# A squared-ReLU MLP whose second product is made by Strassen's seven products for two of three token groups

## The chip, the cores and the metric

One core of a Trainium2 chip runs the whole program. The metric is the time of one execution on the device in microseconds (us); lower is better. The engines are named as the profile names them: PE (matrix products; PEld is its weight load), DVE, ACT and POOL (elementwise work), SP (issues transfers). A row such as `128x512 f32` is 128 partitions by 512 elements each.

## The reference

A two-part layer over 2176 tokens (17 tiles of 128): a mixer (a gated recurrence and chunk-band attention), then the MLP. Only the MLP is touched, and it is about half of the time:

```
x = x + concat(o_h, o_a) @ w_out
u = rmsnorm(x, norm2_g) @ w_up            # 1024 -> 4096
x = x + square(relu(u)) @ w_down          # 4096 -> 1024
y = rmsnorm(x, final_norm_g)
```

All data are float32. Every product of two matrices is made as three: each operand is split into a rounded part (`hi`) and the rest (`lo`), and hi·hi, hi·lo and lo·hi are summed (`mm3`, L365). A split is one cast on ACT and one subtraction on DVE (`wsplit`, L313, for weights).

## The kernel before

The mixer writes its output x1 to device memory and the MLP (`phase_mlp`, L1145) works through the tokens in three groups of 6, 6 and 5 tiles (`GROUPS_M`, L31). The group's normalised activations lie transposed and split in SBUF (`h_hi`, `h_lo`); `prepare` (L1096) makes them, for the first group beside the last of the mixer's output projection, for the others beside the group before.

Per group a loop runs over 16 slices of 256 of the 4096 hidden columns. One slice is:

- **up**: 4 PSUM groups (2 blocks of 128 columns by 2 halves of the tokens), each 24 matmuls of 384 columns (320 for the group of 5 tiles). ACT takes relu (L1178), DVE squares (L1179), ACT casts (L1181), DVE subtracts (L1182).
- **down**: for each token tile and each half of the 1024 output columns one PSUM group of 6 matmuls of 512 columns, which DVE adds to the accumulator y in SBUF (L1201).

Weights come from device memory as 512 KB pieces (`wraw`, two buffers) and are split into `whi`/`wlo` pieces of 512 columns, of which eight lie in SBUF; `wseq` (L344) loads one weight ahead of its use. The final norm of a finished tile (`finish`) is DVE's L125 and a store. Four PSUM buffers (`c.ps_mm`) rotate under up and down.

`weave` mixes two streams of work at trace time by given costs: the MLP of group 0 with the decode requests' attention (`sample_mixer`) and the preparation of group 1, the MLP of group 1 with the preparation of group 2. The order of the instructions on each engine is then fixed when the program is built: a scheduler walks a model of the engines and takes, of the instructions that are ready in it, the one that comes first in the program. So the order on an engine isn't the program's, but it doesn't change at run time either.

Of the kernel before, what the change touches and what calls it, by code (L numbers as in the profile page):

```python
# [17 lines left out]
P = 128  # L18
# [85 lines left out]
def rows(c, prompt, sample, t):  # L104
    return prompt[t * P:(t + 1) * P, :] if t < NPT else sample
# [179 lines left out]
    c.wsp = s.enter_context(c.tc.tile_pool(reuse_waits="tile", name="wsp", bufs=bufs))  # L285


RAW, PIECE = 1024, 512


class W:


    def __init__(self, c, w, ncol=WC, pool=None):
        nc = c.nc
        self.p = []
        self.kp = kp = PIECE // ncol
        for r0 in range(0, w.shape[1], RAW):
            raw = c.wraw.tile([P, RAW], F32, tag="wraw", name="wraw")
            nc.sync.dma_start(out=raw, in_=w[:, r0:r0 + RAW])  # L300
            for o in range(0, RAW, PIECE):
                rw = raw[:, o:o + PIECE]
# [5 lines left out]

    def lo(self, k, s):
        return self.p[k // self.kp][1][:, k % self.kp, s]  # L310


def wsplit(c, rw, pool=None):  # L313
# [7 lines left out]
    nc.scalar.copy(h, rw)  # L321
    nc.vector.tensor_tensor(out=l, in0=rw, in1=h.bitcast(F32), op=ALU.subtract)  # L322
    return hi, lo


class W2(W):
# [16 lines left out]

def wseq(c):  # L344

    srcs = []
    for _ in GROUPS:
        srcs += [(c.w_in[4:6], 0), (c.w_in[4:6], 1)] + [(c.w_in[i], WC) for i in (2, 3, 0, 1)] + \
            [(c.w_in[6:8], 0), (c.w_in[6:8], 1)]
    for kind, _ in TODO:  # L350
        srcs += [(c.w_in[i], WC) for i in (12, 8, 9, 10, 11, 13)] if kind == "p" else \
            [(c.w_out[i], WC) for i in range(D // WC)]
    for _ in GROUPS_M:
        for fc in range(DFF // WC):
            srcs += [(c.w_up[fc], WC), (c.w_down[fc, 0], 512), (c.w_down[fc, 1], 512)]
    w = W2(c, *srcs[0])
    yield None
    for x in srcs[1:]:
        nxt = (W2 if len(x[0].shape) == 3 else W)(c, *x)
        yield w  # L360
        w = nxt
    yield w


def mm3(c, ps, pairs, parts=1):  # L365
# [776 lines left out]
            yield 0.12 * w  # L1142


def phase_mlp(c):  # L1145
    tc, nc = c.tc, c.nc
    GMAX = max(len(g) for g in GROUPS_M) * P
    FC = WC
    with ExitStack() as s:
        def pool(name, bufs, **k):  # L1150
            return s.enter_context(tc.tile_pool(reuse_waits="tile", name=name, bufs=bufs, **k))
        cp = pool("m_const", 1)
        yp = pool("m_y", 7)
        up = pool("m_u", 1)
        wp = pool("m_u2", 2)
        c.ps_mm = pool("m_psmm", 4, space=PSUM)
        c.ps_tx, c.ps_tx_tag = pool("m_pstx", 2, space=PSUM), "tx"
        c.ps_smp = pool("m_pssmp", 2, space=PSUM)
        c.g2 = gain_tile(c, cp, "g2", c.norm2_g)
        gf = gain_tile(c, cp, "gf", c.final_g)  # L1160

        pend = []

        def finish(t, y):
            norm_rows(c, y, gf, y, "y")
            nc.sync.dma_start(out=rows(c, c.y_p, c.y_s, t), in_=y)

        def mlp(tiles, g):
            n = len(tiles) * P
            ys = []  # L1170
            for fc in range(DFF // FC):
                wu = next(c.ws)
                uh = up.tile([P, FC // P, GMAX], F32R, tag="uh", name="uh")
                ul = up.tile([P, FC // P, GMAX], F32R, tag="ul", name="ul")
                for f, cs, ps in proj_fm(c, wu, g, n, 1):
                    cn = cs.stop - cs.start
                    u2 = wp.tile([P, 384], F32, tag="u2", name="u2")[:, :cn]
                    nc.scalar.activation(u2, ps, AF.Relu)  # L1178
                    nc.vector.scalar_tensor_tensor(out=u2, in0=ps, scalar=0.0, in1=u2,  # L1179
                                                   op0=ALU.max, op1=ALU.mult)  # L1180
                    nc.scalar.copy(uh[:, f, cs], u2)  # L1181
                    nc.vector.tensor_tensor(out=ul[:, f, cs], in0=u2, in1=uh.bitcast(F32)[:, f, cs],  # L1182
                                            op=ALU.subtract)
                    for x in pend[:2]:
                        finish(*x)
                    del pend[:2]
                if not fc:
                    for t in tiles:
                        y = yp.tile([P, D], F32, tag="y", name="y")
                        nc.sync.dma_start(out=y, in_=c.x1[t * P:(t + 1) * P, :])  # L1190
                        ys.append(y)
                wd = [next(c.ws), next(c.ws)]
                full = slice(0, 512)
                for j, y in enumerate(ys):
                    ts = slice(j * P, (j + 1) * P)
                    for dc, w in enumerate(wd):
                        ps = c.ps_mm.tile([P, 512], F32, tag="mm", name="mm")
                        list(mm3(c, ps, [(uh[:, k, ts], ul[:, k, ts], w.hi(k, full), w.lo(k, full))
                                         for k in range(FC // P)]))
                        ysl = y[:, dc * 512:(dc + 1) * 512]  # L1200
                        nc.vector.tensor_tensor(out=ysl, in0=ps, in1=ysl, op=ALU.add)  # L1201
                    if fc == DFF // FC - 1:
                        if g.last and pend:
                            finish(*pend.pop())
                        pend.append((tiles[j], y))
                yield 1.0
            if g.last:
                finish(*pend.pop())

        h1 = Ctx()  # L1210
        c.h0.last = h1.last = False

        def side():
            yield from sample_mixer(c)
            h_tiles(pool("m_h", 1), h1)
            yield from prepare(c, GROUPS_M[1], h1)

        run(weave(mlp(GROUPS_M[0], c.h0), 17.0, side(), 26.0))
        run(weave(mlp(GROUPS_M[1], h1), 17.0, prepare(c, GROUPS_M[2], c.h0), 5.0))
        c.h0.last = True  # L1220
        run(mlp(GROUPS_M[2], c.h0))


@with_exitstack
def hymba_kernel(ctx, tc, x_prompt, x_sample, state_hgrn, cache_k, cache_v, lb_param, norm1_g, w_in,
# [19 lines left out]
    c.x1 = dram.tile([NTT * P, D], F32, name="x1")  # L1245
    c.sq, c.sk = (dram.tile([4, P, P], F32, name=x) for x in ("sq", "sk"))
    c.sv = dram.tile([P, 512], F32, name="sv")
    c.ws = wseq(c)
# [4 lines left out]
    wpools(c, ctx, 8, 2, 3)  # L1253
# [73 lines left out]
```

## Time and profile before

| | |
|---|---|
| median of 3 runs | 2972.8 us (2971.18 to 2977.19) |
| the profiled execution, its own time | 2972.54 us |
| its span, first to last instruction | 2970.8 us |
| around the span | 1.7 us |
| PE busy | 2891.7 us (97%) |
| DVE, ACT, POOL busy | 1752.2, 1111.0, 288.1 us |
| MLP's matmuls | from 1373.5 us to about 2957 us of the span |

The profiled execution lies 0.3 us under the median. A busy PE is not PE at its peak: matmuls overlap, so the price of one is the distance of the starts of two in a row, not its length.

### The profile page before, as it was taken

Reading aid. Unit: us, or ns where it says so; the run is one execution under the profiler, and the core shown is the slowest. Engines: PE = TensorE matmul, PEld = TensorE weight load, DVE = VectorE, ACT = ScalarE, POOL = GpSimd, SP = SyncE. Lnnn points to the kernel's source line nnn. Section 1 sums busy time; section 2 is a strip of 40 time slices with the busy share of each in tenths; the row PEclk is TensorE's granted clock in tenths of the full one; section 3 lists DMA queues with packets and bytes.
Section 4 is the critical chain, followed back from the end, with each engine's and each line's share of the span. In section 5 each row is a group of like instructions: output and inputs, shape, how many; then the busy total and the mean of one; then the engine's idle time right before and its main releaser. Section 6 shows DMA issues by size and latency. Waiting matters only on the chain.

```text
span 2970.8 us, 45500 instructions
## 1 busy us (share of the span) xinstructions
PE 2891.7 (97%) x18151; PEld 2626.6 (88%) x18151; DVE 1752.2 (59%) x3110; ACT 1111.0 (37%) x2256; POOL 288.1 (10%) x474
## 2 busy tenths in 40 slices
PE   8999999989999999998999999999999999999997
PEld 7888889889889899898888999999999999899997
DVE  5775775765556565656555555565555555555554
ACT  5433443435545455554223333332222223323222
POOL 3311321221010101011000000010000000000000
PEclk9999999999999999999999999999999999999999
DMA  7433323434333434447322332242212123222221
GB/s 268 163 126 113 113 97 102 137 107 140 100 125 107 128 106 140 141 156 268 114 85 87 117 98 79 72 148 65 78 57 71 57 71 128 82 75 73 84 72 64
DMA packets 119262, 328.06 MB, mean 110 GB/s; under 512 B 12613, under 2 KB 36937, under 8 KB 119050
## 3 DMA queue, kind: packets, MB, share of 16 engines
q1 hardware_dynamic: 110714, 299.20, 31.0%
q0 software_dynamic: 6320, 18.62, 1.6%
q10 hardware_dynamic: 2016, 7.34, 0.7%
q8 instruction: 142, 2.33, 0.3%
q14 instruction: 70, 0.57, 0.1%
HBM read 292.61 MB, written 32.51 MB: 109 GB/s over the span
## 4 chain that ended last, share of the span: by engine, by line
PE 73%; DVE 1%; ACT 1%; DMA 1%; issue 1%; POOL 0%; POOLq 0%; ACTq 0%; DVEq 0%
PE mm L370 22%; PE mm L372 21%; PE mm L371 21%; PE ps_oT L826 3%; PE S L819 2%; PE S L797 2%; PE tx L115 1%; ACT s L810 1%; PE ps_os L888 0%; DMA x<-x 0%; ACT junk L100 0%; DVE s L808 0%; PE tr L835 0%; ACT whi L321 0%; DVE wlo L322 0%
## 5 line engine op out<-in xcount | busy, mean ns | idle before, releaser
L321 ACT CAST whi<-wraw 128x512 fp32r<-128x512 f32 x816 | 498.0, 620 | 747.0 <-PE mm L372 537.2
L322 DVE TENSOR_TENSOR wlo<-wraw,whi 128x512 fp32r<-128x512 f32 x816 | 563.9, 708 | 238.2 <-ACT whi L321 234.3
L1201 DVE TENSOR_TENSOR y<-mm,y 128x512 f32<-128x512 f32 x544 | 373.7, 689 | 221.1 <-PE mm L372 219.4
L370 PE MATMUL mm<-h_hi,whi 128*128 128x384 f32 (+1 forms) x1536 | 503.2, 328 | 0.0
L372 PE MATMUL mm<-h_hi,wlo 128*128 128x384 f32 (+1 forms) x1536 | 501.5, 326 | 0.0
L371 PE MATMUL mm<-h_lo,whi 128*128 128x384 f32 (+1 forms) x1536 | 500.7, 326 | 0.0
L372 PE MATMUL mm<-whi,ul 128*128 128x512 f32 x1088 | 424.1, 390 | 0.0
L371 PE MATMUL mm<-wlo,uh 128*128 128x512 f32 x1088 | 424.0, 390 | 0.0
L370 PE MATMUL mm<-whi,uh 128*128 128x512 f32 x1088 | 423.5, 389 | 0.0
L370 PEld LDWEIGHTS mm<-h_hi,whi 128*128 128x128 f32 x1536 | 288.4, 188 | 4.7 <-issue 3.5
L371 PEld LDWEIGHTS mm<-h_lo,whi 128*128 128x128 f32 x1536 | 288.4, 188 | 1.2
L372 PEld LDWEIGHTS mm<-h_hi,wlo 128*128 128x128 f32 x1536 | 288.4, 188 | 0.0
L1179 DVE SCALAR_TENSOR_TENSOR u<-mm,u 128x384 f32<-128x384 f32 (+1 forms) x192 | 102.4, 534 | 278.4 <-ACT u L1178 278.3
L370 PE MATMUL mm<-hT_hi,whi 128*128 128x384 f32 (+1 forms) x768 | 259.7, 338 | 5.6 <-ACT qs L1003 4.1
L372 PE MATMUL mm<-hT_hi,wlo 128*128 128x384 f32 (+1 forms) x768 | 254.0, 331 | 0.2
L371 PE MATMUL mm<-hT_lo,whi 128*128 128x384 f32 (+1 forms) x768 | 253.4, 330 | 0.0
L372 PEld LDWEIGHTS mm<-whi,ul 128*128 128x128 f32 x1088 | 204.2, 188 | 43.1 <-DVE ul L1182 0.5
L370 PEld LDWEIGHTS mm<-whi,uh 128*128 128x128 f32 x1088 | 204.2, 188 | 41.7 <-ACT uh L1181 0.5
L371 PEld LDWEIGHTS mm<-wlo,uh 128*128 128x128 f32 x1088 | 204.2, 188 | 41.2
L1178 ACT ACTIVATE u<-mm 128x384 f32<-128x384 f32 (+1 forms) x192 | 90.4, 471 | 344.9 <-PE mm L372 344.9
L370 PE MATMUL mm<-whi,hT_hi 128*128 128x256 f32 x720 | 213.4, 296 | 0.5 <-ACT hT_hi L117 0.2
L90 POOL TENSOR_SCALAR r<-ss 128x1 f32<-128x1 f32 (+1 forms) x85 | 24.0, 283 | 1900.7 <-ACT junk L100 1675.7
(206 smaller groups left out, 4641.6 us busy)
## 6 DMA issues: line engine op xcount, KB each, us to landing
wraw<-in_w_in SPq DMA_DIRECT2D x168, 512.0 KB, 4.1
wraw<-in_w_up SPq DMA_DIRECT2D x96, 512.0 KB, 3.8
wraw<-in_w_down SPq DMA_DIRECT2D x96, 512.0 KB, 3.7
wraw<-in_w_out SPq DMA_DIRECT2D x48, 512.0 KB, 3.9
xT<-in_x_T SPq DMA_DIRECT2D x34, 512.0 KB, 4.2
og<-og SPq DMA_DIRECT2D x17, 512.0 KB, 3.5
x<-yo POOLq DMA_DIRECT2D x68, 128.0 KB, 3.3
x<-x SPq DMA_DIRECT2D x17, 512.0 KB, 4.7
```

What stands on the lines that cost most here:

```text
L115: nc.tensor.transpose(ps[:, k, :], src[:, (k0 + k) * P:(k0 + k + 1) * P], c.ident)
L321: nc.scalar.copy(h, rw)
L322: nc.vector.tensor_tensor(out=l, in0=rw, in1=h.bitcast(F32), op=ALU.subtract)
L370: nc.tensor.matmul(ps, lh, rh, start=(i == 0), stop=False)
L371: nc.tensor.matmul(ps, lh, rl, start=False, stop=False)
L372: nc.tensor.matmul(ps, ll, rh, start=False, stop=(i == n - 1))
L797: nc.tensor.matmul(S[:, bk, :n], a[es, qc], c.K[ft][es, b, kc], start=(a is q and not b), stop=(a is ql))
L819: nc.tensor.transpose(ps[:, x, :], s[:, x * P:(x + 1) * P], c.ident)
L826: nc.tensor.matmul(poT[64 * e:64 * e + 64, j, :], g.vt[i - nk + 1 + x][:, 64 * h:64 * h + 64], pts[e][:, x, :], start=(x == 0), stop=(x == ...
L1178: nc.scalar.activation(u2, ps, AF.Relu)
L1179: nc.vector.scalar_tensor_tensor(out=u2, in0=ps, scalar=0.0, in1=u2, op0=ALU.max, op1=ALU.mult)
L1201: nc.vector.tensor_tensor(out=ysl, in0=ps, in1=ysl, op=ALU.add)
```

## The change

The groups become 5, 6 and 6 tiles. Group 0 keeps the plain scheme. In groups 1 and 2 a step covers 512 hidden columns: the activations form a 2 by 2 block matrix (two halves of the tokens, 3 tiles each, by two blocks of 256 hidden columns), the weights another (two blocks of 256 by two halves of the 1024 output columns), and Strassen's scheme (in Winograd's form) makes seven block products of 3 PSUM groups each instead of eight. Each product has its own accumulator (`acc`, in SBUF), which DVE fills with the first step and adds to in the others; after the last step `sums` on DVE joins the seven. The last step of group 2 is done in the plain scheme.

The sums of activations (`comb`, four per step) run on POOL; seven operands instead of four blocks are split (`usplit`). The four sums of weights are made once, for both groups: `Quarters` loads quarters of `w_down`, sums them on POOL, splits them and stores them to device memory (`c.td`); `WT` loads them back, already split, as the weights of four of the seven products. The quarters' loads go through SP and wait for a one-element copy on POOL (`c.touch`) that reads a value which has just left PSUM. They run two steps ahead: the first two steps' sums in group 0, the other six steps' in group 1.

The normalised activations of groups 1 and 2 are no longer kept in SBUF when they are made: `prepare_away` stores them to device memory, and `fetch` loads them in 16 transfers when the group before is done with `h_hi`/`h_lo`. `wseq` now fills all of the eight weight pieces ahead of use instead of one weight.

```diff
-GROUPS_M = [list(range(0, 6)), list(range(6, 12)), list(range(12, 17))]
+GROUPS_M = [list(range(0, 5)), list(range(5, 11)), list(range(11, 17))]
+class Quarters:
+    def __init__(self, c, pool, i, k):
+        self.c, self.pool, self.i = c, pool, i
+        self.ks = slice(k * PIECE, (k + 1) * PIECE)
+        raw = pool[0].tile([P, 4 * PIECE], F32, tag="bq", name="bq").rearrange("p (q x) -> p q x", q=4)
+        c.nc.gpsimd.tensor_copy(raw[0:1, :, 0], c.touch[0:1, 0:4])
+        self.b = [raw[:, q, :] for q in range(4)]
+        for q in range(4):
+            c.nc.sync.dma_start(out=self.b[q], in_=c.w_down[2 * i + q // 2, q % 2][:, self.ks])
+    def sums(self):
+        b = self.b
+        for o, x, y in ((0, 1, 0), (1, 3, 1), (3, 3, 0), (2, 3, 2)):
+            self.c.nc.gpsimd.tensor_tensor(out=b[o], in0=b[x], in1=b[y], op=ALU.subtract)
+    def away(self):
+        for n, x in enumerate((0, 3, 1, 2)):
+            for d, y in zip(self.c.td[self.i][n], wsplit(self.c, self.b[x], self.pool[1])):
+                self.c.nc.gpsimd.dma_start(out=d[:, self.ks], in_=y.bitcast(F32))
+class WT(W):
+    def __init__(self, c, d):
...
+                c.nc.sync.dma_start(out=x.bitcast(F32), in_=y[:, o:o + PIECE])
...
+                srcs += [one(c.w_up[2 * i]), one(c.w_up[2 * i + 1])]
+                for x in ((0, 0), (1, 0), 0, 3, 2, 1, (1, 1)):
+                    if isinstance(x, tuple):
+                        srcs.append((2, lambda a=2 * i + x[0], b=x[1]: W(c, c.w_down[a, b], 512)))
+                    else:
+                        srcs.append((2, lambda i=i, x=x: WT(c, c.td[i][x])))
+    def fill(cur):
+        nonlocal at, used
+        while at < len(srcs) and cur + used + srcs[at][0] <= NPIECE:
+            ahead.append((srcs[at][0], srcs[at][1]()))
...
+def fetch(c, g, hd, ks=range(KT)):
+    if not ks[0]:
+        h_tiles(c.h0p, g)
+    for k in ks:
+        for d, x in zip(hd, (g.hi, g.lo)):
+            c.nc.sync.dma_start(out=x.bitcast(F32)[:, k, :], in_=d.rearrange("p (k n) -> p k n", k=KT)[:, k, :])
...
+                    extra.extend([[lambda: load(0)], [lambda: qs[0].sums()], [],
+                                  [lambda: qs[0].away(), lambda: load(1)], [lambda: qs[1].sums()], [],
+                                  [lambda: qs[1].away()]])       # one entry per PSUM group of up
+                def step(i):
...
+                    for kh in range(2):
+                        up(next(c.ws), g, GMAX, lambda f, cs: a[cs.start // HALF][kh][:, f, :], use)
+                    def comb(out, p, q, op):
+                        nc.gpsimd.tensor_tensor(out=out, in0=p, in1=q, op=op)
+                    comb(a[0][0], a[0][0], a[1][0], ALU.subtract)
+                    comb(a[1][0], a[1][0], a[1][1], ALU.add)
+                    ops.append(usplit(a[1][0]))
...
+                    for p in range(7):
+                        w = next(c.ws)
+                        h, l = ops[p]
+                        for j in range(3):
+                            ts = slice(j * P, (j + 1) * P)
+                            ps = c.ps_mm.tile([P, 512], F32, tag="mm", name="mm")
+                            list(mm3(c, ps, [(h[:, k, ts], l[:, k, ts], w.hi(k, full), w.lo(k, full))
+                                             for k in range(2)]))
+                            if i:
+                                nc.vector.tensor_tensor(out=acc[p][j], in0=ps, in1=acc[p][j], op=ALU.add)
...
+                                    nc.sync.dma_start(out=x1[j], in_=c.x1[t * P:(t + 1) * P, :])
...
+                        after(p)
+                        if i == NF - 1 and nxt and p in (1, 3):
+                            nxt(range(0, 4) if p == 1 else range(4, 8))
```

(`ops[0]` and `ops[1]` are split while up runs; `after(p)` makes the operand of product p+3. The `x1` loads stand in the first step of a group, for products 1, 3 and 6.)

## Rows read from the trace of the kernel before

**Rows 1.** The page's first part: busy time, share of the span, instructions.
```profile
span 2970.8 us, 45500 instructions
PE 2891.7 (97%) x18151; PEld 2626.6 (88%) x18151; DVE 1752.2 (59%) x3110; ACT 1111.0 (37%) x2256; POOL 288.1 (10%) x474
```

**Rows 2.** Busy time by stretch; the columns are named in the first row.
```profile
core 0: us, PE busy (x) PEld busy (x) DVE busy (x) ACT busy (x) POOL busy (x), PEclk, DMA share, GB/s
2200.00:2300.00 100.00, 100.00 (x514) 91.38 (x513) 53.69 (x87) 27.38 (x50) 0.00 (x0) 1.00 0.20 64
2600.00:2700.00 100.00, 100.00 (x565) 91.44 (x564) 55.43 (x95) 29.68 (x58) 0.00 (x0) 1.00 0.24 75
```

**Rows 3.** All that PE waited for from 1380 to 2960 us.
```profile
PE mm L370 <- ACT sT_hi L117: 2.3, 3, 1.8
PE mm L372 <- DVE sT_lo L118: 0.4, 2, 0.2
```

**Rows 4.** PE in order of time: start, length, line; group 1 of the MLP.
```profile
1969.82 0.39 PE L371 MATMUL mm<-wlo,uh 128*128 128x512 f32 x1
...
1977.52 0.39 PE L372 MATMUL mm<-whi,ul 128*128 128x512 f32 x1
...
1978.82 0.33 PE L370 MATMUL mm<-h_hi,whi 128*128 128x384 f32 x1
...
1982.98 0.33 PE L370 MATMUL mm<-h_hi,whi 128*128 128x384 f32 x1
```

**Rows 5.** Groups of instructions by shape, 1800 us to the end: busy, mean ns.
```profile
L1201 DVE TENSOR_TENSOR y<-mm,y 128x512 f32<-128x512 f32 x420 | 288.4, 689 | 168.3 <-PE mm L372 166.6
L322 DVE TENSOR_TENSOR wlo<-wraw,whi 128x512 fp32r<-128x512 f32 x292 | 197.6, 688 | 55.3 <-ACT whi L321 54.4
L321 ACT CAST whi<-wraw 128x512 fp32r<-128x512 f32 x292 | 181.1, 622 | 426.3 <-PE mm L372 383.5 <-PE mm L371 33.5 <-DMA wraw<-in_w_up 3.2
L1182 DVE TENSOR_TENSOR ul<-u,uh 128x384 fp32r<-128x384 f32 x84 | 46.8, 557 | 22.6 <-ACT uh L1181 22.6
L1179 DVE SCALAR_TENSOR_TENSOR u<-mm,u 128x384 f32<-128x384 f32 x84 | 46.7, 556 | 135.0 <-ACT u L1178 134.9
L1181 ACT CAST uh<-u 128x384 fp32r<-128x384 f32 x84 | 43.0, 512 | 47.8 <-DVE u L1179 47.8
L1178 ACT ACTIVATE u<-mm 128x384 f32<-128x384 f32 x84 | 41.1, 490 | 165.6 <-PE mm L372 165.6
```

**Rows 6.** POOL's lines: min/median/max ns of one.
```profile
L484 POOL TENSOR_TENSOR gate<-gate,hgain x17: 1253/1308/2208, 99.1 to 597.6; 128x512 f32<-128x512 f32 x17
L194 POOL TENSOR_TENSOR xT<-xT,g x31: 1887/1899/2661, 19.5 to 1155.4; 128x1024 f32<-128x1024 f32 x31
```

**Rows 7.** POOL's groups by line: busy, mean ns of one.
```profile
L956 POOL DMA_DIRECT2D x<-yo x68 | 38.0, 559 | 324.2 <-DVE yo L955 287.4 <-DMA x<-x 32.7 <-DMA og<-og 4.0
```

**Rows 8.** DVE in order of time, twice four weight splits.
```profile
8.40 2.49 DVE L322 TENSOR_TENSOR wlo<-wraw,whi 128x512 fp32r<-128x512 f32 x4
...
112.81 4.19 DVE L322 TENSOR_TENSOR wlo<-wraw,whi 128x512 fp32r<-128x512 f32 x4
```

**Rows 9.** POOL in order of time, beside the second of these.
```profile
113.87 1.98 POOL L194 TENSOR_TENSOR xT<-xT,g 128x1024 f32<-128x1024 f32 x1
```

**Rows 10.** Stretches of 5 us around the MLP's start; columns as in rows 2.
```profile
1375.00:1380.00 5.00, 3.59 (x22) 3.44 (x22) 2.79 (x5) 1.55 (x3) 1.64 (x3) 1.00 1.00 352
1380.00:1385.00 5.00, 5.00 (x30) 5.00 (x30) 1.40 (x3) 1.50 (x3) 0.00 (x0) 1.00 1.03 419
1385.00:1390.00 5.00, 5.00 (x31) 5.00 (x30) 1.40 (x3) 1.47 (x4) 0.00 (x0) 1.00 1.04 381
```

**Rows 11.** Transfers by line: issuer, count, size, median us to landing.
```profile
wraw<-in_w_down SPq DMA_DIRECT2D x96, 512.0 KB, 3.7
og<-bias POOLq DMA_DIRECT2D x16, 256.0 KB, 3.9
```

**Rows 12.** PE in order of time at the MLP's start.
```profile
1374.81 0.34 PE L371 MATMUL mm<-h_lo,whi 128*128 128x384 f32 x1
1376.56 0.66 PE L115 MATMUL tx<-ident,x 128*128 128x128 f32 x4 [1.41 <-DVE h_lo L118]
```

More of the change, by code (lines that the diff above doesn't have):

```diff
@@ L1147, in phase_mlp @@
     GMAX = max(len(g) for g in GROUPS_M) * P
[L1148 to L1169, printed above, removed]
-            ys = []
[L1171 to L1187, printed above, removed]
@@ new lines, in phase_mlp, with finish, up @@
+    pend, later, extra = [], [], []
+    EARLY = 2
+    def finish(t, y):
+        norm_rows(c, y, gf, y, "y")
+        nc.sync.dma_start(out=rows(c, c.y_p, c.y_s, t), in_=y)
+    def up(wu, g, n, dst, use=None):
+        for f, cs, ps in proj_fm(c, wu, g, n, 1):
+            u = dst(f, cs)
+            nc.scalar.activation(u, ps, AF.Relu)
+            nc.vector.scalar_tensor_tensor(out=u, in0=ps, scalar=0.0, in1=u, op0=ALU.max, op1=ALU.mult)
+            if use:
+                use(f, cs, u)
+            c.touch = u
+            for todo in (later, extra):
+                for x in todo.pop(0) if todo else ():
+                    x()
@@ new lines, in plain @@
+    def plain(g, tiles, ys, dst, usplit, at, then=None):
+        n = len(tiles) * P
+        up(next(c.ws), g, n, dst, usplit)
+        if then:
+            then()
+        wd = next(c.ws)
+        for j, y in enumerate(ys()):
+            for dc, w in enumerate(wd):
+                ps = c.ps_mm.tile([P, 512], F32, tag="mm", name="mm")
+                list(mm3(c, ps, [at(k, j) + (w.hi(k, full), w.lo(k, full)) for k in range(2)]))
+                ysl = y[:, dc * 512:(dc + 1) * 512]
+                nc.vector.tensor_tensor(out=ysl, in0=ps, in1=ysl, op=ALU.add)
+            yield j
@@ L1188, in mlp @@
                     for t in tiles:
-                        y = yp.tile([P, D], F32, tag="y", name="y")
+                        y = py.tile([P, D], F32, tag="y", name="y")
                         nc.sync.dma_start(out=y, in_=c.x1[t * P:(t + 1) * P, :])
                         ys.append(y)
[L1192 to L1205, printed above, removed]
@@ L1206, in mlp @@
-                yield 1.0
-            if g.last:
-                finish(*pend.pop())
[L1210 to L1221, printed above, removed]
+                return ys
@@ new lines, in group0, with then @@
+            NF = DFF // WC
+            qs = []
+            for fc in range(NF):
+                def then():
+                    if qs:
+                        qs.pop().away()
+                    u = fc - (NF - 2 * EARLY - 1)
+                    if 0 <= u < 2 * EARLY:
+                        qs.append(Quarters(c, pq, u // 2, u % 2))
+                    if fc == NF - 1:
+                        nxt()
+                for j in plain(g, tiles, get, dst, usplit, at, then):
+                    pass
+                if qs:
+                    qs[0].sums()
+                yield 1.0
@@ new lines, in phase_mlp, with side @@
+    h1, h2 = Ctx(), Ctx()
+    def side():
+        yield from sample_mixer(c)
+        with ExitStack() as s:
+            yield from prepare_away(c, pool(s, "m_st0", 2), GROUPS_M[1], c.hd[0])
+    with base:
+        run(weave(group0(c.h0, GROUPS_M[0], lambda: fetch(c, h1, c.hd[0])), 16.0, side(), 26.0))
+        w = wino([(h1, GROUPS_M[1], lambda ks: fetch(c, h2, c.hd[1], ks)), (h2, GROUPS_M[2], None)])
+        sp = next(w)
+        run(weave(w, 32.0, prepare_away(c, sp, GROUPS_M[2], c.hd[1]), 16.0))
@@ L1247, in hymba_kernel @@
     c.sv = dram.tile([P, 512], F32, name="sv")
+    c.hd = [[dram.tile([P, HN], F32, name=f"hd{i}{x}") for x in ("hi", "lo")] for i in range(2)]
+    c.td = [[[dram.tile([P, 1024], F32, name=f"t{i}{n}{x}") for x in ("hi", "lo")] for n in range(4)]
+            for i in range(DFF // 512)]
     c.ws = wseq(c)
```

197 lines of the change are left out of this document (182 added, 15 removed).

## The prediction

> **What bounds the kernel now.** I read the page first: PE is busy for 97% of the span, DVE for 59%, ACT and POOL for less [rows 1]. As a busy PE can still have slack, I then read three things of the MLP alone. By stretches, PE is busy for all of 2200 to 2300 and 2600 to 2700 us at a granted clock of 1.00 (its 2.4 GHz level), while DVE does 54 us of 100, ACT 27 to 30, POOL nothing, and transfers take 20 to 24% of the DMA time [rows 2]. The view of PE's waits from 1380 to 2960 us has two entries, 2.7 us together, both from the decode requests' projection [rows 3]. And the starts of matmuls in a row are even: 34 distances in 7.70 us, so 0.2265 us per matmul of 512 columns, and 24 in 4.16 us, so 0.1733 us per matmul of 384 [rows 4]. So the MLP lasts as long as its matmuls take one after another; nothing else in it sets the time, and a matmul less is worth its whole distance. What has room is named by the same rows: DVE 46%, ACT 70%, POOL 100%, DMA 76%.
>
> **What the change removes.** Two slices of 256 hidden columns take 2 × 6 tiles × 2 halves × 6 = 144 matmuls of 512 columns for down; seven products of 3 PSUM groups of 6 take 126. The 18 saved are worth 18 × 0.2265 = 4.08 us a step, one product. Steps that change: 8 in group 1, 7 in group 2, so 15 × 4.08 = 61.2 us. Up is the same work (17 tiles; only the group with 5 moves from last to first), and so are the transposes of 17 tiles.
>
> **One tile leaves the crowded start.** `prepare` now makes five tiles instead of six beside the mixer's last projection. PE waits there for the tiles' splits, 1.41 us before one set of transposes, for example [rows 12]; the tile's PE work goes into group 0, where it costs the same. One wait of that size less: 1.5 us gained (0 to 3).
>
> **What it adds to the other engines, per step of 61.8 us** (up 8 × 24 × 0.1733 = 33.3, products 7 × 4.08 = 28.5). Durations are the rows of 384 and 512 elements [rows 5], and for 768 elements the line through them: DVE 0.96 us, ACT 0.84 us. POOL's 768 lie between 1.31 (512) and 1.90 us (1024) [rows 6]; I take 1.6.
> - DVE in group 1: 21 adds × 0.69 = 14.5; 8 squares × 0.556 = 4.4; 7 subtractions of operands × 0.96 = 6.7; splits of weights (8 up, 6 down, 8 of the sums) 22 × 0.69 = 15.2. Sum 40.8, 66%. In group 2 the 8 splits of the sums are missing: 35.3, 57%.
> - ACT: 8 × 0.49 + 7 × 0.84 + 22 × 0.62 = 23.4, 38%.
> - POOL: 4 combinations × 1.6 + 8 sums × 1.31 + 16 issues of transfers × 0.56 [rows 7] = 25.8, 42%.
> - Transfers in group 1: up 2.1 MB, three raw weights 1.6, four sums read 4.2, quarters read 2.1 and stored 4.2, the next group's tile 1.6: 15.7 MB a step, 254 GB/s. The trace's full stretches moved 352 to 419 GB/s [rows 10], so 61 to 72% of what it can.
>
> None of them reaches 100%, so no engine replaces PE as an average. I cost this work at nothing in itself; what covers it is PE's products, and what it costs without that cover is in the terms and rivals below.
>
> **Contention of POOL with DVE.** The trace bears on it: four weight splits take 2.49 us alone and 4.19 us when a POOL operation of 1.98 us falls into them [rows 8, 9]; the 1.70 us of excess is nearly all of it. POOL's reading operations in a step of group 1 are 4 × 1.6 + 8 × 1.31 = 16.9 us, so DVE has at most 40.8 + 16.9 = 57.7 us of 61.8, if all of it fell on splits. I take it as covered, with little to spare. The Trainium skill, page "SBUF — State Buffer", section "Who interferes with whom", states the rule behind it, and it speaks against this change: a VectorE instruction with two SBUF inputs and a GpSimd instruction that reads SBUF exclude each other for the whole of an instruction. The trace agrees with 1.70 of 1.98 us. By the rule the adds from PSUM, which have one SBUF input, would stay free; by its worst case the step still ends under 61.8 us.
>
> **The chain inside a step.** Products 0 and 1 use operands that are split while up runs, so from the end of up PE has 8.16 us of work before product 2 needs its own. That operand comes from the last PSUM group of up: relu 0.49, square 0.56, two combinations on POOL 3.2, cast 0.84, subtraction 0.96: 6.1 us, 2.1 less than the cover. The later operands have two products of time as well and shorter chains (at most 1.6 + 0.84 + 0.96 = 3.4 us). If product 2 were late, DVE's adds stand behind the same subtraction in its fixed order, and PE fills the other three PSUM buffers (4.1 us) and stops. A POOL sum of 1.31 us or an issue of 0.56 in front of the combinations fits into 2.1 us; two or three don't. I take 0.4 us a step, 6 us in all (0 to 4 us a step as bounds).
>
> **Weights of the products.** A sum's pieces are 1.05 MB, wanted 4.08 us after one another: 257 GB/s for four products. Eight pieces of buffer let them be asked for three products (12.2 us) ahead; 512 KB lands in 3.7 us and 256 KB issued by POOL in 3.9 [rows 11]. Even with the stores of sums (2.1 MB) in front, 4.2 MB at 352 GB/s is 12 us: just covered, nothing added.
>
> **The change of groups.** `fetch` brings 6.3 MB when the last up of a group is done, where before the next group's activations lay in SBUF.
> - Group 0 to 1: with 1 MB of weights 7.3 MB at about 380 GB/s (the middle of the three [rows 10]), 19 us, and 3.7 until the first lands [rows 11], 23 us in all. Cover: 60 matmuls of down, 13.6 us, and 7/8 of up's first PSUM group, 3.6, as the blocks arrive in the order of use. 5 us left (0 if PE begins several PSUM groups, 9 at 352 GB/s with the sums' stores).
> - Group 1 to 2: behind it 5.8 MB of weights for five products and the next up: 12.1 MB, 32 + 4 us, against 28.5 + 3.6: 4 us (0 to 8).
>
> The Trainium skill, page "DMA: Bandwidth & Descriptors", section "Where 436 GB/s comes from", has about 358 GB/s as the limit between device memory and SBUF. The trace exceeds it with 419 over 5 us; by 358 the two terms would come to 8 and 6 us in place of 5 and 4.
>
> **First steps of groups 1 and 2.** Nine loads of x1 (512 KB each) go through SP behind weights, and DVE's evacuation of products 1, 3 and 6 waits for them. 1.6 MB for three takes 4.1 us and 3.7 to land, against 4.1 us of PSUM ahead and a product's time: up to 3.7 us a time where SP is late. I take 1.5 us a group, 3 us (0 to 10). The joining sums after a group (6 DVE operations a tile, 4.7 us, three tiles) lie under the next up's 33 us with a PSUM group every 4.16 us: nothing. The end, a norm and a store after the last product, is as it was.
>
> **The sum**, from the profiled execution (2972.5, of which 2970.8 is the span; 0.3 under the median): 2972.5 − 61.2 − 1.5 + 6 + 5 + 4 + 3 = 2927.8, so 2928 us.
>
> **Rivals.**
> 1. **All is covered.** The chains keep their 2.1 us, PE starts the new group's up on several PSUM groups: 2972.5 − 61.2 − 1.5 = 2910. For it: PE waited 2.7 us in 1580 us of MLP [rows 3]. Against: DVE and DMA had twice the room then.
> 2. **POOL and DVE exclude each other** in the six steps of group 1 that make sums: the subtraction of product 2's operand comes 6 us late, PSUM hides some, PE waits 4 us: 6 × 4 = 24 us more, 2952. For: the 1.70 us [rows 8, 9], and PE's order is fixed, so it waits at one instruction though others are ready (1.41 us in [rows 12]). Against: it needs three or more POOL operations in front.
> 3. **Slower: the chain through POOL in every step.** The place is product 2's operand. A step is longer than two old slices once PE waits more than 4.08 us in it, which is when the chain of 6.1 us takes over 8.16 + 4.08 = 12.2 us. With 14 us (each combination behind two sums or splits) the cost is 15 × 1.8 = 27 us: 2972.5 + 27 = 3000. For: nothing in the old trace has a chain ACT, DVE, POOL, ACT, DVE under PE. Against: in group 2 POOL has only the combinations.
> 4. **The loads aren't spread.** The quarters wait on SP for POOL's copy, and with them the weights behind; if that order is bad, product 2 waits for its weights, about 4 us a step as well, and the gain is gone: 2972.
>
> **Chances.** Forecast 0.60 (2915 to 2943 its own range); all covered 0.12; POOL and DVE 0.14; gone within 0.2% 0.04; slower by the chain or by the loads 0.10. Differences under 0.2%, 6 us, can't be told from none in this kernel. Faster 0.60 + 0.12 + 0.14 = 0.86, same 0.04, slower 0.10. The range reaches from just below rival 1 to past rival 2, where each of the 15 steps loses 2.9 us instead of 0.4: 2921.8 without any + 15 × 2.9 = 2966. So 2908 to 2966.
>
> **What the profile after would show.** Right: matmuls of 512 columns down by 15 × 18 = 270 from 6 per PSUM group at the same 0.2265 us; steps of 61.8 us in group 2 and little more in group 1; PE's waits in the MLP of some 15 to 20 us, most at the two changes of group and named as waits for h_hi or for weights; POOL near 40% and DVE near 66% in group 1. Wrong: waits of PE for uh/ul or for a PSUM buffer in each step (rivals 2 and 3), or for whi/wlo loads of the sums (rival 4), a granted clock under 1.00 inside steps, or matmuls farther apart than 0.2265 us.

## The result and the profile after

The changed kernel takes 3000.1 us (median of 4 runs, 2995.1 to 3005.8), against 2974.8 us for the kernel before on the same chip. The ratio is 1.0086 with a 95% interval of 1.0073 to 1.0099: slower by 0.9%, where 2928 us was forecast. The profiled execution (3005.8 us) is the slowest of its four.

The page of the changed kernel, parts 1 and 2 (one line of the latter):

```profile
span 3004.0 us, 46416 instructions
## 1 busy us (share of the span) xinstructions
PE 2862.7 (95%) x17881; PEld 2592.7 (86%) x17881; DVE 1804.1 (60%) x3092; ACT 1158.1 (39%) x2295; POOL 593.7 (20%) x754
...
PE   8999999989999999999999999988888999999998
```

Set beside [rows 1], PE works 29 us less, and the span is 33 us longer. The 62 us of both together are time in which PE stands, most of it in the slices with an 8 behind the middle. Where it stands is plain in the stretches. The first row is the part of group 1 that makes weight sums, the second is five undisturbed steps of group 2:

```profile
core 0: us, PE busy (x) PEld busy (x) DVE busy (x) ACT busy (x) POOL busy (x), PEclk, DMA share, GB/s
1945.00:2363.00 418.00, 366.20 (x1770) 324.53 (x1770) 249.36 (x342) 139.56 (x242) 169.40 (x188) 0.93 0.66 224
2555.00:2865.00 310.00, 310.00 (x1594) 285.19 (x1593) 166.62 (x253) 90.04 (x148) 40.22 (x20) 1.00 0.40 131
```

Group 2 is as [rows 2]: PE without a gap at a granted clock of 1.00. In group 1 PE misses 52 of 418 us, the clock is 0.93, and no other engine is near full: DVE 60%, ACT 33%, POOL 41%, DMA 66%. So nothing has become the bound by its amount of work. Something comes late. The waits of the same 418 us, for PE, ACT and POOL (us in total, times, longest):

```profile
PE mm L433 <- DVE a L1266: 42.7, 7, 9.6
PE mm L433 <- ACT e L1412: 3.9, 2, 2.9
PE mm L433 <- DVE e L1410: 2.3, 3, 1.4
...
ACT whi L344 <- POOL bq L328: 107.2, 23, 10.7
...
POOL bq L320 <- DVE a L1266: 52.2, 5, 22.5
POOL bq L328 <- DMA bq<-in_w_down: 46.5, 11, 6.5
```

[rows 3] had 2.7 us of PE's waits in the whole MLP. Here PE waits for DVE's squares (L1266), that is for a PSUM buffer of up. (L1412 is ACT's copy of a product into its accumulator: in the first step ACT fills three of the seven accumulators, and DVE the others.) At the same time ACT stands before the cast of a weight sum (L344) until POOL has made the sum (L328), and POOL stands until the quarters have landed. One such stall, in the third step of group 1, engine by engine (start, duration, engine, line, what, and in brackets the idle time before it and who ended it):

```profile
2095.84 0.18 POOL L320 COPY bq<-a 1x4 f32<-1x4 f32 x1
2102.48 1.27 POOL L328 TENSOR_TENSOR bq<-bq 128x512 f32<-128x512 f32 x1 [6.46 <-DMA bq<-in_w_down]
2105.28 1.27 POOL L328 TENSOR_TENSOR bq<-bq 128x512 f32<-128x512 f32 x1
...
2096.05 2.56 SPq L323 DMA_DIRECT2D bq<-in_w_down  x4
...
2103.79 0.62 ACT L344 CAST whi<-bq 128x512 fp32r<-128x512 f32 x1 [10.68 <-POOL bq L328]
2108.38 0.62 ACT L344 CAST whi<-bq 128x512 fp32r<-128x512 f32 x1 [3.97 <-POOL bq L328]
2110.26 0.62 ACT L344 CAST whi<-bq 128x512 fp32r<-128x512 f32 x1 [1.26 <-DVE wlo L345]
2110.78 0.48 ACT L1265 ACTIVATE a<-mm 128x384 f32<-128x384 f32 x1
...
2094.93 1.01 DVE L1266 SCALAR_TENSOR_TENSOR a<-mm,a 128x384 f32<-128x384 f32 x2
2104.44 0.69 DVE L345 TENSOR_TENSOR wlo<-bq,whi 128x512 fp32r<-128x512 f32 x1 [8.51 <-ACT whi L344]
2111.65 0.69 DVE L345 TENSOR_TENSOR wlo<-bq,whi 128x512 fp32r<-128x512 f32 x1 [1.42 <-DMA t40lo<-wlo]
2112.26 0.55 DVE L1266 SCALAR_TENSOR_TENSOR a<-mm,a 128x384 f32<-128x384 f32 x1
...
2112.86 0.80 PE L433 MATMUL mm<-whi,uh 128*128 128x512 f32 x1 [9.65 <-DVE a L1266]
2113.46 0.63 PE L434 MATMUL mm<-wlo,uh 128*128 128x512 f32 x1
2113.89 0.63 PE L435 MATMUL mm<-whi,ul 128*128 128x512 f32 x1
...
2116.38 0.39 PE L434 MATMUL mm<-wlo,uh 128*128 128x512 f32 x1
2116.60 0.39 PE L435 MATMUL mm<-whi,ul 128*128 128x512 f32 x1
2116.83 0.40 PE L433 MATMUL mm<-whi,uh 128*128 128x512 f32 x1
```

Read it from POOL. The touch runs at 2095.84, the quarters' load goes out from 2096.05 on, and POOL's first sum starts 6.4 us later; POOL makes the four sums; ACT casts them one by one, DVE subtracts, and the subtraction also waits for the store of an earlier one, as there are two buffers. Three of these casts and subtractions stand ahead of the relu (L1265) and square (L1266) of up's seventh PSUM group. (In the program they follow that square: they are the seventh and last entry of `extra`, which has one per PSUM group of up. So it is the scheduler that has put them in front.) By the even pace of up that PSUM group was complete at about 2096.4; its relu starts at 2110.78, its square at 2112.26. PE fills the PSUM buffers that it has, stands for 9.65 us, and begins again with matmuls 0.43 us and more apart; only from the eighth on are they 0.23 us apart.

To place the losses I took, from the timeline of PE, the start of the first matmul of each up and of each set of products. A step of group 2 is 33.3 + 28.6 = 61.9 us (forecast: 61.8). In group 1 the ups keep to 33.4 us apart from the first two. The products of its first six steps, beside sums, take 43.7, 41.8, 42.9, 40.3, 40.0 and 39.4 us; those of the last two, without sums, 28.6.

### The profile page after: what moved, and what is told of

Its sections match the earlier page's. It is cut to its first block, busy times and chain, and to the rows that moved or that the text cites. A ratio compares the mean times of both kernels' runs of the same rounds, so it can differ in the third digit from the quotient of the medians.

```text
span 3004.0 us, 46416 instructions
## 1 busy us (share of the span) xinstructions
PE 2862.7 (95%) x17881; PEld 2592.7 (86%) x17881; DVE 1804.1 (60%) x3092; ACT 1158.1 (39%) x2295; POOL 593.7 (20%) x754
## 4 chain that ended last, share of the span: by engine, by line
PE 58%; DMA 7%; DVE 4%; POOL 4%; issue 3%; ACT 2%; SPq 0%; POOLq 0%; ACTq 0%; DVEq 0%
PE mm L433 17%; PE mm L435 16%; PE mm L434 16%; DMA bq<-in_w_down 3%; PE ps_oT L889 3%; PE S L882 2%; POOL bq L328 2%; PE S L860 2%; DVE wlo L345 1%; DMA x<-x 1%; ACT whi L344 1%; ACT s L873 1%; ACT junk L100 1%; DMA h_hi<-hd0hi 1%; PE ps_os L951 0%
## 5 line engine op out<-in xcount | busy, mean ns | idle before, releaser
L344 ACT CAST whi<-wraw 128x512 fp32r<-128x512 f32 x786 | 475.6, 619 | 487.4 <-PE mm L435 291.6
L433 PE MATMUL mm<-whi,uh 128*128 128x512 f32 x998 | 400.0, 401 | 62.0 <-DVE a L1266 42.7
L434 PE MATMUL mm<-wlo,uh 128*128 128x512 f32 x998 | 396.1, 397 | 0.2 <-DMA wlo<-t00lo 0.2
L435 PE MATMUL mm<-whi,ul 128*128 128x512 f32 x998 | 395.6, 396 | 0.0
L433 PEld LDWEIGHTS mm<-whi,uh 128*128 128x128 f32 x998 | 191.7, 192 | 113.0 <-DVE a L1266 47.4
L435 PEld LDWEIGHTS mm<-whi,ul 128*128 128x128 f32 x998 | 191.6, 192 | 41.9 <-DVE ul L1306 1.0
L434 PEld LDWEIGHTS mm<-wlo,uh 128*128 128x128 f32 x998 | 192.1, 192 | 39.6 <-DMA wlo<-t00lo 1.0
L1385 POOL TENSOR_TENSOR a<-a 128x768 f32<-128x768 f32 x60 | 120.0, 2001 | 457.9 <-DVE a L1266 395.0
L435 PE MATMUL mm<-whi,hT_lo 128*128 128x256 f32 x720 | 208.8, 290 | 1.0 <-DVE hT_lo L118 1.0
L434 PE MATMUL mm<-wlo,hT_hi 128*128 128x256 f32 x720 | 207.5, 288 | 0.0
```

Source lines behind the costliest of these rows:

```text
L433: nc.tensor.matmul(ps, lh, rh, start=(i == 0), stop=False)
L434: nc.tensor.matmul(ps, lh, rl, start=False, stop=False)
L435: nc.tensor.matmul(ps, ll, rh, start=False, stop=(i == n - 1))
L1385: nc.gpsimd.tensor_tensor(out=out, in0=p, in1=q, op=op)
```

## Experiments

The time of a run also holds the spread of the mixer, which runs before the MLP. The first up matmul of the MLP starts at 1377.65 us here and at 1366.84 us in the first experiment, though PE's order of work is the same until long after that point. So each run is given with the MLP's length as well, from that first matmul to the end of the span: 1597.3 us before (2970.8 − 1373.5) and 1626.4 us after (3004.0 − 1377.65). Without any loss the change would leave 1597.3 − 61.2 = 1536.1. The MLP's length and the products are those of the profiled execution, also where the time is a median. The first six experiments have one run each, and four runs of one kernel differ by up to 15 us in time (e8), so small differences between them show nothing.

| kernel | time, us | MLP, us | products of group 1's six first steps, us |
|---|---|---|---|
| changed kernel, profiled execution | 3005.8 | 1626.4 | 39.4 to 43.7 |
| e1_nosums | 2923.2 (one run) | 1554.6 | 28.6 to 29.4 |
| e2_bare | 2933.3 (one run) | 1562.9 | 39.6, then 29.4 |
| e4_notouch | 3018.8 (one run) | 1639.3 | 43.8 to 49.3 (four), then 29.4 |
| e5_tied | 2976.5 (one run) | 1603.0 | 36.3 to 39.0 |
| e6_tied_inplace | 2955.3 (one run) | 1580.7 | 33.8 to 37.4 |
| e7_inplace | 2989.1 (one run) | 1614.3 | 36.6 to 44.7 |
| e8_early | 2953.1 (median) | 1582.0 | 37.7, then 29.4 |
| e9_spaced | 2931.0 (median) | 1559.5 | 35.3, then 29.4 |
| e10_spaced4 | 2934.3 (median) | 1562.0 | 36.2, then 29.4 |
| e11_free_first | 2921.5 (median) | 1548.5 | 28.6, then 29.4 |
| e12_prep_later | 2918.0 (median) | 1546.7 | 28.6, then 29.4 |

29.4 is 28.6 and the 0.8 us of transposes of a tile of group 2 (the first tile's stand in the second up, so the first products have none). **The theory**: what costs the time is where the sums' instructions stand in the fixed orders. **The rivals**: the transfers, the tie of the loads, or the amount of work on POOL and DVE.

**e1_nosums: no weight sums in group 1** (its steps 2 to 7, and those of group 2, take the sums of steps 0 and 1):

```diff
-                        srcs.append((2, lambda i=i, x=x: WT(c, c.td[i][x])))
+                        srcs.append((2, lambda i=i, x=x: WT(c, c.td[i % 2][x])))
...
-                    if g is gs[0][0] and i + EARLY < NF:
+                    if False:
                         quarters(i + EARLY)
```

> Group 1 makes no weight sums: its steps and group 2's read the sums of the first two steps again, so the loads of the products are the same in size and number, and the output's values are not the reference's. Theory A (the sums' casts and subtractions stand in ACT's and DVE's fixed order ahead of the last PSUM groups of up, and wait there for the quarters' load, the POOL sums and the stores): the seven products of the first six steps of group 1 take 28.6 us as in group 2, not 39.4 to 43.7; 76 us less, about 2922 to 2930 in all. Theory B (the loads of the split sums and the next group's preparation crowd the transfers): half of the loss stays, 2955 or more. Theory C (POOL's combinations of activations are too slow for product 2 in group 1): the loss stays, 2990 or more.

The MLP is 71.8 us shorter, and the products of group 1 take 28.6 or 29.4 us (29.7 in the last step, where the next group's activations are fetched). So the sums, with their loads and stores, cost the 72 us, and the seven products with their combinations, operand splits and loads of ready sums cost nothing beyond their matmuls. Group 0's last four slices, which still make sums, lose as before. The first up of group 1 takes 33.6 us, the second 36.8.

**e2_bare: the sums' transfers without their arithmetic.** Loads, touch and 16 stores a step stay; the POOL sums, casts and subtractions are left out in group 1, and the raw quarters are stored.

```diff
     def sums(self):
+        if self.bare:
+            return
...
     def away(self):
+        if self.bare:
+            for n, x in enumerate((0, 3, 1, 2)):
+                for d in self.c.td[self.i][n]:
+                    self.c.nc.gpsimd.dma_start(out=d[:, self.ks], in_=self.b[x])
+            return
```

> Group 1 keeps the quarters' loads, their tie and all 16 stores a step with the same bytes, but the stored data are the raw quarters: no sums on POOL, no casts and subtractions of them (output's values not the reference's). Theory A: nothing of the sums stands in ACT's or DVE's order, so the products take 28.6 us, 2922 to 2935. Theory B (transfers): the products stay at 38 us or more, 2980 or more. Theory D (the loads behind the tie hold up the weights on SP): also 2980 or more, with waits of PE for weights.

From the second step on the products take 29.4 us with the DMA engines at 75% from 1945 to 2300 us. The transfers are covered, except in group 1's first step, where 11 us are lost with no sum made, of the 15 that the changed kernel loses there; the last two runs come back to that step.

**e4_notouch: loads not tied to PSUM.**

```diff
-        c.nc.gpsimd.tensor_copy(raw[0:1, :, 0], c.touch[0:1, 0:4])
```

> The change without the one-element copy that ties a quarter's load to a value that left PSUM; all work is done. Theory A: the loads start when the buffer is free and the data lie ready when the casts are due, but the second load of a step still follows the first's splits: products of 33 to 38 us, 2960 to 2985. Theory E (the tie is what spreads the sums and keeps the loss down): longer than the change, 3010 or more. Theory B: no difference, 3000.

The MLP grows by 13 us: 3018.8 us, as theory E had it and not theory A (2960 to 2985). In group 1 the sums crowd into the first four steps (43.8 to 49.3 us), and the last two of the six are free of loss; the six together take 245.8 us, against 248.0. The 13 us are group 0's, which takes 546.1 us instead of 533.4: without the tie POOL makes its sums at 1406 to 1499 us, beside the decode requests, and its second to fourth slice lose 27 us, while the downs of its last four take 13.6 us each. So the tie isn't the culprit, but it ties only the loads. Nothing ties the casts and subtractions behind them.

**e5_tied: casts tied as well.** A copy of four elements of a value that has just left PSUM goes into the cast's target first; a set of quarters is cast in two halves, from three PSUM groups after its load on.

```diff
+            if tie:
+                nc.scalar.copy(hi[0:1, 0:4], self.c.touch[0:1, 0:4])
+            nc.scalar.copy(hi, self.b[x])
...
-                                  [lambda: qs[0].away(), lambda: load(1)], [lambda: qs[1].sums()], [],
-                                  [lambda: qs[1].away()]])
+                    extra.extend([[lambda: rest(A)], [], [lambda: rest(B), lambda: load_sum(0)], [], [],
+                                  [lambda: put(0, A)], [], [lambda: put(0, B), lambda: load_sum(1)]])
```

> All work is done; in group 1 the casts of the sums are tied too, each by a four-element copy on ACT of a value that left PSUM, three PSUM groups of up (12.5 us) after their load, and in two halves two PSUM groups apart, so that the third and fourth piece don't wait for the stores of the first two in the two split buffers. Theory A: the data are there when the casts' turn comes, and up's last PSUM groups are not behind them: products near 28.6 to 32 us, 2925 to 2945. Theory B (transfers): no change, 2990 to 3005. Theory F (POOL and DVE exclude each other): DVE's and POOL's work is the same, so most of the loss stays, 2980 or more.

The MLP loses 23 us less than in the changed kernel, but 2976.5 us is well over the 2925 to 2945 that theory A expected. What is left is of another kind. In ACT's timeline the tie now stands in front of the next operand's cast (L1367) and waits for a store to free its buffer:

```profile
2226.90 0.48 ACT L1273 ACTIVATE a<-mm 128x384 f32<-128x384 f32 x1
2231.92 0.19 ACT L337 CAST whi<-a 1x4 fp32r<-1x4 f32 x1 [4.54 <-DMA t60hi<-whi]
2233.97 0.19 ACT L337 CAST whi<-a 1x4 fp32r<-1x4 f32 x1 [1.86 <-DMA t61hi<-whi]
...
2235.11 1.56 ACT L1367 CAST uh<-a 128x768 fp32r<-128x768 f32 x2
```

**e6_tied_inplace and e7_inplace: more buffers for the casts.** The low part is written over the sum, so that the space of the low parts gives four buffers of high parts. e6 keeps the ties, e7 is the changed kernel's own order with the same buffers.

```diff
-            nc.vector.tensor_tensor(out=lo, in0=self.b[x], in1=hi.bitcast(F32), op=ALU.subtract)
+            nc.vector.tensor_tensor(out=b, in0=b, in1=hi.bitcast(F32), op=ALU.subtract)
...
-            pq = pool(s, "m_q", 1), pool(s, "m_qs", 2)
+            pq = pool(s, "m_q", 1), pool(s, "m_qs", 4)
```

> The tied casts of the run before, and the low part of a sum is written over the sum itself instead of a second buffer; the room goes to two more buffers for the high part (four), so no cast in group 1 waits for a store. Theory A in two parts (part 1: casts due before load and sums are there, cured by the tie; part 2: the third and fourth cast wait for the stores of the first two): products of the first six steps fall from 36.3 to 39.0 us to 29 to 32, about 2935 to 2945 in all. If part 2 isn't it (the later casts wait for POOL's sums instead), products stay over 35 us, 2970 or more.

> The change with the in-place low part and four high buffers in group 1, but without the tie of the casts. Theory A, part 2 alone: the stores' wait goes, the wait for load and sums stays: products of 35 to 40 us, 2970 to 2990. If the stores' wait were all of it: 29 to 32 us and 2935 to 2945. If the casts' place in ACT's order is all of it: no change, 2995 or more.

The MLP loses 46 us less than in the changed kernel with both, 12 with the buffers alone, 23 with the ties alone. By these single runs the parts help each other: a tie to the right place gains more if it then has a buffer. e6's 2955.3 us is still over the 2935 to 2945 expected: each of the six sets of products loses 4 to 9 us, and POOL's and ACT's timelines say why. Sums and low parts now share their memory, so the next load has to wait for the store:

```profile
2202.26 0.18 POOL L320 COPY bq<-a 1x4 f32<-1x4 f32 x1 [5.94 <-DMA t53lo<-bq]
...
2206.23 1.29 POOL L328 TENSOR_TENSOR bq<-bq 128x512 f32<-128x512 f32 x1 [1.87 <-DMA bq<-in_w_down]
...
2207.55 0.62 ACT L337 CAST whi<-bq 128x512 fp32r<-128x512 f32 x1 [3.23 <-POOL bq L328]
2210.77 0.62 ACT L337 CAST whi<-bq 128x512 fp32r<-128x512 f32 x1 [2.60 <-POOL bq L328]
```

The load is 6 us late, and the casts meet up's last PSUM groups again.

**e8_early: seven of eight steps' sums in group 0**, tied, with three buffers there.

```diff
-    EARLY = 2
+    EARLY = 7
...
-                        qs.pop().away()
+                        qs.pop().away(range(4), True)
```

> As the tied in-place run, but fourteen of the sixteen half sums are made in group 0, one per slice of 27.7 us (load at the end of an up, casts tied to the end of the next), and only the last two in the first steps of group 1. Theory A: a cast then never waits, as load, sums and stores have a whole slice: group 1's products take 28.6 to 29.4 us from the third step on, group 0's slices lose under 1 us each; 2915 to 2930. Rival (the loss moves with the work, wherever the sums are made: transfers, POOL against DVE): 14 slices lose 2 to 6 us each as in the change's group 0, 2945 to 2980.

2953.1 us, ratio to the kernel before 0.9925 (0.9901 to 0.9950), and in the rival's band. Group 1 is nearly clean, but group 0 takes 25 us more than in e6 (552.9 instead of 527.9 us). Nineteen of them lie in its fourth to sixth slice, where PE waits for elementwise work of the decode requests (L945, L947), which shares DVE with the sums. PE's waits from 1450 to 1580 us, 7.2 us of the nineteen (what makes up the rest was not placed):

```profile
PE tr L951 <- DVE pz L947: 3.9, 3, 2.4
PE tr L951 <- DVE pz L945: 3.3, 3, 1.5
```

So moving the sums moved the loss, as it would by either theory: an order that fits one place doesn't fit the other. This run didn't tell them apart.

**e9_spaced: the same work, put where it fits.** A step makes one set of quarters between up's second and sixth PSUM group, the other between product 2, behind the last combination, and product 6. In group 0 the sums are tied as in e8.

```diff
+                    extra.extend([[], [lambda: load_sum(0)], [], [], [lambda: put(0, A)], [lambda: put(0, B)]])
+                    return {2: lambda: load_sum(1), 5: lambda: put(1, A), 6: lambda: put(1, B)}
...
                         after(p)
+                        if p in late:
+                            c.touch = acc[p][0]
+                            late[p]()
```

> The kernel with tied casts and the low part written over the sum lost 5 us in the products of each of group 1's six first steps, because the load of the second set of quarters still waits for the first set's stores (5.9 us) and its sums then stand in front of product 2's combination and of the last squares. Here a step makes its first set between up's second and sixth PSUM group and its second set between product 2 and product 6, when the combinations of the operands are done; nothing else is changed. Theory (the loss is the order only, the work itself is covered): the six steps' products take 28.6 to 30 us, and with 8 to 14 us lost at the change to group 1 and in group 0 the time is 2920 to 2932. Rival (the work of POOL and DVE doesn't fit under 61.8 us, wherever it stands): products of group 1 stay at 33 us and more, 2945 to 2965.

2931.0 us, ratio 0.987 (0.9849 to 0.989), as the theory expected. From the second step on the products take 29.4 us with every sum, cast, subtraction and store in place. In these steps the amount of work is not the trouble.

**e10_spaced4: four steps' sums in group 0** (`EARLY = 4`).

> The same spacing, with the weight sums of the first four steps (instead of two) made in group 0, so that group 0 makes them in its last eight slices and group 1 in its first four steps. If group 1's steps lose nothing more with the new spacing, this gains nothing: within 6 us of the kernel with two steps' sums in group 0, and more if the decode requests' part of group 0 is held up (0 to 10 us). If each of group 1's steps still loses 3 us or more, two of them are saved here, 6 us and more less.

2934.3 us: no difference, as expected where steps of group 1 lose nothing.

**e11_free_first and e12_prep_later: the crowd at the change to group 1.** e9 lost some 19 us in group 1's first step and second up. e11 leaves the first step without sums; e12 also lets the preparation of group 2 begin a step later.

```diff
-    EARLY = 2
+    EARLY = 3
...
-                    late = quarters(i + EARLY) if g is gs[0][0] and i + EARLY < NF else {}
+                    late = quarters(i + 2) if g is gs[0][0] and 0 < i < NF - 2 else {}
...
+    def next_group(sp):
+        yield 1.0
+        yield from prepare_away(c, sp, GROUPS_M[2], c.hd[1])
```

> The spaced kernel lost 4.2 us in group 1's first up, 6.7 in its first products and 8.4 in its second up; in these 110 us SP, POOL and the x buffers carry the change of groups (16 fetches, group 0's outputs), the first loads of x1, the preparation of group 2's first tiles and a step's weight sums at once. Here group 1's first step makes no weight sums: group 0 makes those of three steps, and steps 1 to 5 make those of the step two ahead. Theory (these losses are the sums' share of the crowd, as in the kernel without sums in group 1, which lost 3.7 us there): 13 to 15 us less, 0 to 6 back in group 0, so 2915 to 2925. Rival (the change of groups itself and the preparation set them): within 5 us of the spaced kernel's 2931.

> The same, and the preparation of group 2's tiles begins one step later, so that its loads don't share the x buffers with the first step's x1. In the spaced kernel PE waited 6.1 us in the second up for the norm of such a tile, and 3.3 us even in the kernel without sums. Theory: 3 to 6 us less than the kernel of the line before, 2911 to 2921. Rival (the wait moves along with the preparation, to the third up): no difference beyond 2 us.

e11: 2921.5 us, first products 28.6 us instead of 35.3, second up 38.1 instead of 41.8. e12: 2918.0 us, second up 33.3 us without a gap, so that wait is gone and hasn't moved. Its first up is 2.8 us longer than e11's, so the two medians, 3.5 us apart and with ranges that overlap, don't separate them. e12 against the kernel before: 0.9817 (0.9801 to 0.9833). The stretch from its second step to its eighth up, the five steps with sums alone (the first five of that stretch), and ACT's and POOL's waits in the whole stretch:

```profile
1966.00:2376.00 410.00, 410.00 (x2149) 379.82 (x2148) 268.07 (x377) 153.79 (x295) 160.15 (x167) 1.00 0.67 223
1966.00:2280.00 314.00, 314.00 (x1630) 288.83 (x1629) 219.57 (x303) 124.38 (x243) 148.12 (x158) 1.00 0.73 246
...
ACT a L1272 <- PE mm L442: 85.5, 35, 3.7
ACT whi L351 <- PE mm L442: 39.0, 16, 2.8
...
POOL bq L328 <- DMA bq<-in_w_down: 45.3, 15, 4.7
```

In the five steps DVE, ACT, POOL and DMA are busier than in the changed kernel (DVE 70%, ACT 40%, POOL 47%, DMA 73%), POOL waits for the quarters nearly as long (45.3 us against 46.5), and PE has no gap at all. What has gone is ACT's 107 us of waiting for POOL (0.6 us are left): ACT's relus now wait for PE, as they should where PE is the bound.

## Why the prediction was wrong

**The saving was right.** 18 matmuls a step at 0.2265 us: a step of group 2 takes 61.9 us for the 61.8 forecast. Of the 61.2 us e12 keeps about 45: from the first up matmul to the end of the last matmul it takes 1536.2 us, the kernel before 1581.0. What it still loses lies at the changes of group and in a few of group 0's slices.

**The step that failed is "I cost this work at nothing in itself; what covers it is PE's products".** I added up what the weight sums put on DVE, ACT and POOL and found each below 100%. These totals were near: DVE 70%, ACT 40%, POOL 47% in e12's five steps, where nothing stalls (forecast 66, 38, 42). But room on an engine covers work only if the work doesn't stand in front of something else and wait. I listed what stands behind the quarters' loads on SP, and never what stands behind the sums' casts on ACT and DVE: the relu and the square that free PSUM. The price by the products: 248.0 us for six sets instead of e1's 28.6 + 5 × 29.4, so 72.4 us, and e1's whole MLP shows 71.8 us by taking the sums out. 50.6 us of it are gaps; in the other 22 us PE works, but at less than its pace, 1.9 us of them behind the stall shown (seven distances in 3.52 us instead of 1.59). Five of the six steps lose 57 us, and there e2 loses nothing once the arithmetic of the sums is left out. The first step's 15 us aren't all of this kind: e2 loses 11 there with transfers alone, and PE waits as long for ACT's copies into the accumulators (3.9 us) as for squares (3.6 us).

The Trainium skill, page "PSUM — Partial Sum Buffer", section "Engine vs sequencer instructions", says that the queues of ScalarE, VectorE and GpSimd are strict FIFO. The trace agrees: the relu of a PSUM group that was complete at about 2096.4 us started 14.4 us later, behind casts that waited. I knew that the order is fixed and used it for PE alone. Why the scheduler put the casts there was not measured; that its model took the sums as ready earlier than they were is only argued, from the effect of the ties.

Group 0's last four slices add 14.0 us: downs of 20.0, 15.7, 16.3 and 16.5 us instead of 13.6. PE waits there mostly for ACT's cast of down's own operand (L1305, 7.8 us). With the sums' casts tied, e9 loses 2.2 us in these slices.

**The chain inside a step** (6 us forecast) was the wrong chain. Its own parts came out a little longer than I took them (a combination 1.8 to 2.5 us for 1.6), and it cost nothing: in e12's stretch of 410 us PE doesn't wait for it once.

**Rivals.** Rival 3 named 3000 us, and the median is 3000.1, by coincidence: it had each of 15 steps lose 1.8 us at product 2's operand, where six steps lost 10 to 15 us each, most of it at up's last PSUM groups, and group 2's steps after the first nothing. It said nothing of the weight sums' own casts. (Waits of PE for a PSUM buffer, the sign that the prediction gave for rivals 2 and 3, did come, but the buffer was one of up's.) Rival 2, exclusion of POOL and DVE, is refuted as a cause of the loss: both are busier in e12. Its mark is seen, as subtractions of 512 elements take 0.85 us in the mean beside POOL's sums (0.69 in group 2's undisturbed steps) and the sums up to 2 us, but it is covered. Rival 4, weights held up on SP, is refuted: in the whole MLP PE waited 0.2 us for a load of ready sums and 1.7 us for splits of weights.

**The tile that leaves the crowded start** (−1.5 us) can't be read: where the MLP starts varies by 11 us between executions with the same order on PE. PE's wait for the splits from 1300 us on is 7.0 us, as against 6.4 before.

**The changes of group and first steps** (5 + 4 + 3 us) were near, though the first 5 was a slip: its own terms, 19.3 + 3.7 − 17.2, give 5.8 (and the 8 us that it sets beside them comes to about 7). Group 0 to 1 cost 3.0 us in the kernel's first two ups (without the 0.8 of transposes), and in e1, whose group 1 makes no sums, as much. Group 1 to 2 cost 3.8 + 3.2 = 7.0 us, of which PE's waits for loads of weights or activations are 0.2 us; DVE waits 5.1 us for x1 there.

**The sum by what was measured**, for the MLP: 1597.3 − 61.2 + 72.4 + 14.0 + 3.0 + 7.0 = 1632.5, against 1626.4. 5.6 of the 6 us too many lie at the very end, which the prediction took as unchanged: from the end of the last matmul to the end of the span the kernel before takes 16.2 us (2954.5, not about 2957, to 2970.8), the changed kernel 10.6. Its last store is issued 3.6 us before the end of the span, that of the kernel before 8.6 us. Why is not shown.

## What to carry to other kernels

Adding busy times up to less than 100% doesn't show that side work is covered. For each new chain, write down what stands behind its waiting instructions on every engine that it uses, not only on the one that starts it: an instruction that waits for a load → POOL → store chain in ACT's or DVE's order stops the evacuation of PSUM, and so PE. A tie that spreads such work must hold every link of it (load, cast, buffer), and the place for a chain is where nothing behind it is needed before it ends: here the sums cost 57 us in five steps where their casts stood ahead of up's last PSUM groups, and nothing in e12's five steps, where half of them stand between up's second and sixth PSUM group and half between the last combination and the last product, with tied casts and four buffers.

## What the runs showed of the hardware

A stall costs more than its length. After 9.65 us without matmuls PE went on at about half its pace (0.43 us from matmul to matmul, against 0.23), and the windows show the granted clock there at 0.50, the 1.2 GHz level, until it rose at about 2116 us:

```profile
2090.00:2100.00 10.00, 10.00 (x60) 10.00 (x59) 5.93 (x8) 1.85 (x4) 4.87 (x7) 1.00 0.88 296
2100.00:2112.00 12.00, 3.22 (x15) 2.36 (x13) 2.25 (x3) 2.24 (x4) 7.72 (x9) 0.75 0.83 313
2112.00:2116.00 4.00, 3.13 (x7) 2.04 (x8) 3.10 (x6) 1.74 (x3) 1.52 (x3) 0.50 0.69 222
2116.00:2120.00 4.00, 3.06 (x12) 2.17 (x12) 1.46 (x3) 1.56 (x2) 1.96 (x2) 0.96 0.89 313
```

In this stretch, with the DMA engines 83 to 88% busy, the four 256 KB loads of quarters took 5.9 to 6.0 us each from issue to landing; [rows 11] had 3.9 us for 256 KB issued by POOL.
